# Four gate pieces behind the first values, rotation copies on two engines, urgent probability copies, and one store from another queue

## The chip, the cores and the metric

The kernel runs on one core of one Trainium2 chip. The time is device microseconds of one execution, the median of three runs: 883.94 us (883.38 to 884.23). The engines are TensorE (PE in the rows), VectorE (DVE), ScalarE (ACT), GpSimd (POOL) and SyncE (SP, which here only issues transfers). Each engine works through its own instructions in the order in which they stand; semaphores tie the engines together.

## The reference

Three layers over 256 tokens of width 1024, in float32:

```
# layer 1: retention
q, k, v, gate = split(x @ a_w_in); q, k = rope(q), rope(k) / 16
x = layer_norm(alpha * x + (norm(retention(q, k, v)) * silu(gate)) @ a_w_out)
# layer 2: latent attention, 16 heads
c = x @ kv_w_down; lat = rms_norm(c[:512]); k_rope = rope(c[512:])
k_nope, v = split(lat @ kv_w_up)
q_nope, q_rope = split(rms_norm(x @ b_w_in[:768]) @ b_w_uq); q_rope = rope(q_rope)
p = softmax(causal(q_nope @ k_nope + q_rope @ k_rope) * scale)
x = layer_norm(alpha * x + (p @ v * silu(x @ b_w_in[768:])) @ b_w_out)
# layer 3: recurrent branch and indexed sparse attention, gated, then a wide feed-forward
x = x + (gate0 * (y_rnn @ w_o_rnn) + gate1 * (y_attn @ w_o_attn)) @ w_out
x = x + square(relu(rms_norm(x) @ w_ff_in)) @ w_ff_out
```

`rope` turns pairs of columns: `x1 * cos - x2 * sin` and `x2 * cos + x1 * sin`.

## The kernel before, in words

All weights stream in as pieces of up to 128x1024 float32. A piece lands in a `raw` buffer (four of them; the small opening pieces land in `t` buffers). The helper `split` (L242) makes two halves of it in a `whl` buffer (eight of them): ScalarE casts it to the high half (L243), VectorE subtracts that from the piece for the low half (L244). Every product of matrices is then three matmuls, high by high, high by low and low by high (`mm3`, L297 to L299). Results gather in PSUM: four accumulators `acc`, two `tr` for transposes, two `att`. A new `acc` tile takes the buffer that falls free next in the program's order, and its first matmul waits until the last reader of that buffer is done.

The order of the instructions on each engine is set when the program is built, by a scheduler that follows the program's order and its own estimate of when things are ready; `urgent` (L208) lets a call go ahead of what is not urgent. Nothing is reordered while the program runs.

Four places matter here.

- **The opening** (`values_and_gates`, L509). Eight slices of the input each bring a piece of `x`, one of the first head's values (`av`) and one of its gates (`ag`). The values gather in two accumulators, the gates in two more, so all four are taken. The gate products of the last `CLOSE` slices are held back and run after the last value product. Then the values are copied out (`split`, named `t2r<-acc` in the rows), which frees an accumulator for the queries of head 0 (`ropeA("aq")`, matmuls `acc<-s,whl`).
- **The rotation in layer 2** (`ropeB`, L702). For the shared key once, and then for each of four groups of four heads. The accumulator `bqr` with the rotary queries is copied in four blocks of 32 partitions with neighbours exchanged (L708), multiplied by the cosines (L710) and sines (L713), and added (L714). L710 is the last reader of the accumulator. A group's `ropeB` stands among the last head's work of the group before.
- **The heads** (`head`, L731, and `mix`, L759). A head's probabilities are turned by three transposes into `tr` (L753), copied out as a high and a low part for the first 256 columns (`split`, L755, `t2r<-tr`) and as plain numbers for the last 128 (L756, `pair<-tr`); `mix` multiplies them with the values (`att<-t2r` and `att<-pair`, L764). Accumulators in a pair of heads are taken in the order `bqr` (first pair of a group only), `bqn`, `bkn`, `bv`, `bg`: the `bg` of a group's first pair takes the buffer that `bqr` had.
- **The end** (`ff_out`, L1255, and `store`, L1285). The last corner of the output is worked out in two halves of 256 columns in `tr` tiles. Each half is summed on VectorE (L1287) and stored (L1288); all five stores are issued from SP.

Of the kernel before, what the change touches and what calls it, by code (L numbers as in the profile page):

```python
# [31 lines left out]
WARM = 9  # L32
OPENING = tuple((k, 1) for k in range(8))
TABLES_AT = 3
CLOSE = 3
STEPS = ("w0 w1 b x0 G00 G01 x1 z0 g0 a x2 G02 z1 g1 a x3 G03 z2 g2 a x4 G04 z3 g3 a x5 G05 z4 g4 a x6 G06 z5 g5 "
         "a x7 G07 z6 g6 a G10 z7 g7 a G11 r G12 G13 a G14 G15 G16 G17 "
         "O00 O01 O02 O03 O04 O05 O06 O07 O10 O11 O12 O13 O14 O15 O16 O17").split()
# [110 lines left out]
def ff_group(g):  # L149
    return range(4) if g == 0 else range(2 * g + 2, 2 * g + 4)  # L150
# [21 lines left out]
def body(ctx, nc, tc, wpk, tabs, cols, rows, wab, xtok, out, start="A", stop="C"):  # L172
# [11 lines left out]
    dma = nc.sync.dma_start  # L184
    V = nc.vector
    A = nc.scalar
# [3 lines left out]
    def acc():  # L190
        return accp.tile([P, 512], F32, tag="acc", name="acc")

    def tr():
        return trp.tile([P, 512], F32, tag="tr", name="tr")

    def att():
        return attp.tile([P, 512], F32, tag="att", name="att")

    def t2():
        return t2p.tile([P, 512], F32, tag="t2", name="t2")  # L200

    def t2r():
        return t2p.tile([P, 512], F32R, tag="t2", name="t2r")

    def sm():
        return smp.tile([P, 16], F32, tag="sm", name="sm")

    def urgent(fn, *args):  # L208
        with tc.high_priority():
            fn(*args)  # L210
# [3 lines left out]
    def transpose(dst, src):  # L214
        flips.append(nc.tensor.transpose(dst, src, ident))  # L215
# [26 lines left out]
    def split(h, l, src):  # L242
        A.copy(h, src)  # L243
        V.tensor_sub(l, src, h.bitcast(F32))  # L244
# [39 lines left out]
    def take(name):  # L284
        for item in later:
            item[0] -= 1
        while later and later[0][0] <= 0:
            later.pop(0)[1]()
        while state["fetch"] < min(state["take"] + 1 + AHEAD, len(pieces)):
            fetch()  # L290
        state["take"] += 1
        got, pc = ready.pop(0)
        assert got == name, (got, name)
        return pc

    def mm3(ps, ah, al, bh, bl, st, sp):
        return [mm(ps, lhsT=ah, rhs=bh, start=st, stop=False),  # L297
                mm(ps, lhsT=ah, rhs=bl, start=False, stop=False),  # L298
                mm(ps, lhsT=al, rhs=bh, start=False, stop=sp)]  # L299
# [16 lines left out]
    def tgemm(name, npieces, act):  # L316

        ps = [None, None]
        k0 = 0
        for i in range(npieces):  # L320
            pc = take(name)
            for t in range(2):
                if i == 0:
                    ps[t] = acc()
                tpart(ps[t][:, :pc.n], pc, act, t, k0, i == 0, i == npieces - 1)
            k0 += pc.nk
        return ps
# [70 lines left out]
    def parts(st, j, i):  # L398

        n = st.shape[1] // 2  # L400
        return st[:, j * n + i * 128:j * n + i * 128 + 128]

    def half_product(ps, st, bh, bl, first=True):


        mm(ps, lhsT=st, rhs=bh, start=first, stop=False)  # L406
        mm(ps, lhsT=st, rhs=bl, start=False, stop=True)  # L407
# [13 lines left out]
    def row(name):  # L421

        i = [r[0] for r in ROWS].index(name)
        o = sum(r[1] for r in ROWS[:i])
        w = ROWS[i][1]
        got = []
        for c in range(0, w, 512):
            n = min(512, w - c)
            r = rowp.tile([P, 512], F32, tag="row", name="row")
            load(r[:, :n], rows[:, o + c:o + c + n])  # L430
            got.append(r[:, :n])
        return got
# [9 lines left out]
    def wide(ap, m):  # L442
        return ap.unsqueeze(1).to_broadcast([P, m, ap.shape[1]])
# [12 lines left out]
    if start == "A":  # L456
# [52 lines left out]
        def values_and_gates():  # L509
# [3 lines left out]
            for i, (k0, nk) in enumerate(OPENING):  # L513
                take("x")
                for nm in ("av", "ag"):
                    pc = take(nm)
                    if nm == "ag" and i >= len(OPENING) - CLOSE:
                        last.append((i, k0, pc))
# [77 lines left out]
    if start == "A":  # L596
        load(xs.rearrange("p t n -> p (t n)"), xtok.rearrange("p t n -> p (t n)"))
        g, b = row("lng0"), row("lnb0")
# [60 lines left out]
    if start in "AB":  # L659
# [37 lines left out]
        ps = tgemm("blat", 4, x1T)  # L697
# [4 lines left out]
        def ropeB(ps, m, dst):  # L702

            n = m * 256
            rot = t2()
            for i in range(4):
                a, b = 32 * i, 32 * (i ^ 1)
                A.copy(rot[a:a + 32, :n], ps[b:b + 32, :n])  # L708
            q = t2()
            V.tensor_mul(q[:, :n].rearrange("p (m n) -> p m n", m=m), ps[:, :n].rearrange("p (m n) -> p m n", m=m),  # L710
                         wide(cosB, m))
            r3 = rot[:, :n].rearrange("p (m n) -> p m n", m=m)
            V.tensor_mul(r3, r3, wide(sinB, m))  # L713
            V.tensor_add(dst, q[:, :n], rot[:, :n])  # L714
# [7 lines left out]
        ps = acc()  # L722
        ftile(ps[:, :256], take("bkr"), 0, x1T)
        ropeB(ps, 1, kr)
        A.copy(krh, kr)
        for j in range(2):
# [4 lines left out]
        def head(j, qn, qhl, qr, qs, pr, kn, khl, pl):  # L731
            c = slice(j * 128, j * 128 + 128)
            ck = slice(j * 256, j * 256 + 256)
            sc = att()
            mm(sc[:, 0:128], lhsT=qn[:, c], rhs=kn[:, c], start=True, stop=False)
            mm(sc[:, 0:128], lhsT=qr[:, pr * 256:pr * 256 + 128], rhs=krz[:, j], start=False, stop=True)
            mm3(sc[:, 128:384], qhl[:, 0, j], qhl[:, 1, j], khl[0][:, ck], khl[1][:, ck], True, False)
            half_product(sc[:, 128:384], parts(qs, j, pr), krh, krl[:, j], first=False)
            s = sm()
            pb = t2()  # L740
            for t, c in CT:
                V.tensor_tensor_reduce(out=pb[:, c], in0=sc[:, c], in1=maskB[:, c], scale=1.0,
                                       scalar=GONE, op0=ALU.add, op1=ALU.max, accum_out=s[:, t:t + 1])
            V.scalar_tensor_tensor(s[:, 2:4], s[:, 0:2], -1.0, sq, op0=ALU.mult, op1=ALU.mult)
            for t, c in CT:
                A.activation(out=pb[:, c], in_=pb[:, c], func=AF.Exp, scale=sq[:, t:t + 1],
                             bias=s[:, 2 + t:3 + t], accum_out=s[:, 4 + t:5 + t])
            V.reciprocal(s[:, 6:8], s[:, 4:6])
            for t, c in CT:
                V.tensor_scalar(pb[:, c], pb[:, c], s[:, 6 + t:7 + t], None, op0=ALU.mult)  # L750
            pp = tr()
            for i in range(3):
                transpose(pp[:, i * 128:i * 128 + 128], pb[:, i * 128:i * 128 + 128])  # L753
            pt = t2r()
            split(pt[:, 0:256], pt[:, 256:512], pp[:, 0:256])  # L755
            A.copy(pl, pp[:, 256:384])  # L756
            return pt, pl

        def mix(h, j, pt, vs, v, u):  # L759
# [9 lines left out]
        for g in range(4):  # L769
            if g == 1:  # L770
                softplus()
            ps = acc()
# [6 lines left out]
            for pr in range(2):  # L779
                ps = acc()  # L780
# [8 lines left out]
                ps = acc()  # L789
# [7 lines left out]
                ps = acc()  # L797
# [7 lines left out]
                ps = acc()  # L805
# [39 lines left out]
    if start in "AB":  # L845
        g, b = row("lng1"), row("lnb1")
# [129 lines left out]
    for g in range(4):  # L976
# [8 lines left out]
        for j in range(2):  # L985
            i = 2 * g + j
# [27 lines left out]
    for c in range(2):  # L1014
        ps = tgemm("cq", 4, hT)
# [239 lines left out]
    def ff_out(g):  # L1255
        hh = hid.pop(g)
        ms = range(len(ff_group(g)))
        pcs = [take("fo") for _ in ms]
        if g == NFG - 1:
            rest = t2()  # L1260
            V.scalar_tensor_tensor(rest, fps[1][1], r3[:, 1:2], xs[:, 1, 512:1024], op0=ALU.mult, op1=ALU.add)
        for t in range(2):
            tk = slice(t * 128, t * 128 + 128)
            for n in range(2):
                c = slice(n * 512, n * 512 + 512)
                corner = t == n == 1
                if corner and g == NFG - 1:
                    continue
                for m in ms:
                    mm3(fps[t][n], hh[:, 0, m, tk], hh[:, 1, m, tk], pcs[m].h[:, 0, c], pcs[m].l[:, 0, c],  # L1270
                        g == 0 and m == 0, g == NFG - 1 - corner and m == ms[-1])
                if g == NFG - 1:
                    store(t, c, fps[t][n], xs[:, t, c])
        if g < NFG - 1:
            return

        for i in range(2):
            c = slice(512 + i * 256, 768 + i * 256)
            ps = tr()[:, 0:256]
            for m in ms:  # L1280
                mm3(ps, hh[:, 0, m, tk], hh[:, 1, m, tk], pcs[m].h[:, 0, c], pcs[m].l[:, 0, c],
                    m == 0, m == ms[-1])
            store(1, c, ps, rest[:, i * 256:i * 256 + 256])

    def store(t, c, ps, x):  # L1285
        o = t2()[:, :c.stop - c.start]
        V.scalar_tensor_tensor(o, ps, r3[:, t:t + 1], x, op0=ALU.mult, op1=ALU.add)  # L1287
        dma(out[t * 128:t * 128 + 128, c], o)  # L1288
# [5 lines left out]
    for g in range(NFG):  # L1294
        if g + 1 < NFG:
            ff_in(g + 1)
        ff_out(g)
# [92 lines left out]
```

## Time and profile before

| what | value |
|---|---|
| median of three runs | 883.94 us |
| the profiled execution's own time | 884.91 us |
| its span, first to last instruction | 883.1 us |
| granted TensorE clock over the span | 0.999 |
| PE busy | 874.0 us (99%) |
| DVE busy | 621.1 us (70%) |
| ACT busy | 506.5 us (57%) |
| DMA, from HBM | 154.12 MB, 176 GB/s |

The page's span is shorter than the execution's own time by 1.8 us, which lie outside the first and the last instruction. In a timeline row the first number is the start in us from the beginning of the span, the second how long it took; `x3` means three instructions merged in one row; in brackets stands how long the engine had been idle before, and what ended that. `PE` rows are matmuls, which overlap: the distance between the starts of two of them is the time one takes from the engine.

### The profile page before, as it was taken

To read this page: it belongs to the slowest core of one execution; us is meant where nothing else is said; L and a number is where in the kernel's file an instruction comes from. 1 tells how busy PE (TensorE), PEld (TensorE's weight loads), DVE (VectorE), ACT (ScalarE), POOL (GpSimd) and SP (SyncE) were. 2 spreads that over 40 slices of the span, in tenths; PEclk is the share of its full clock that TensorE was granted. 3 is DMA by queue.
4 is the path that set the end of the run, shared out by engine and by line. 5 is a ranking of instruction groups with operands and counts; after the bars stand their busy time and mean duration, and the time that the engine had idled before them with its cause. 6 is when DMAs were issued, how large, how long until landed. Compare 5 with 4: busy or idle time off the path is not lost.

```text
span 883.1 us, 15178 instructions
## 1 busy us (share of the span) xinstructions
PE 874.0 (99%) x5845; PEld 801.1 (91%) x5845; DVE 621.1 (70%) x1175; ACT 506.5 (57%) x877; POOL 39.9 (5%) x45
## 2 busy tenths in 40 slices
PE   9999999999999999999999999999999999999998
PEld 6988898889999999999888899999999889999997
DVE  6886776757776777777588799777976756555552
ACT  6644445435756666576456678889643455444440
POOL 0000000100100000001311020000000000000000
PEclk9999999999999999999999999999999999999999
DMA  9855455734744444445555534333575556555531
GB/s 319 303 180 168 160 173 171 292 125 156 240 156 153 157 166 145 155 164 198 197 185 180 195 128 143 120 126 115 184 242 195 177 157 215 191 192 191 191 119 48
DMA packets 48313, 156.16 MB, mean 177 GB/s; under 512 B 5488, under 2 KB 7280, under 8 KB 48112
## 3 DMA queue, kind: packets, MB, share of 16 engines
q1 hardware_dynamic: 48240, 155.19, 51.9%
q8 instruction: 46, 0.75, 0.3%
q14 instruction: 27, 0.22, 0.1%
HBM read 154.12 MB, written 1.05 MB: 176 GB/s over the span
## 4 chain that ended last, share of the span: by engine, by line
PE 92%; DVE 5%; ACT 1%; issue 1%; DMA 1%; POOL 0%; SPq 0%; ACTq 0%; DVEq 0%
PE acc L297 24%; PE acc L299 24%; PE acc L298 24%; PE att L297 4%; PE att L298 4%; PE att L299 4%; PE tr L215 3%; DVE whl L244 1%; PE att L1071 1%; DVE s L998 1%; PE acc L1115 1%; DMA t<-wpk 1%; PE att L406 0%; PE att L407 0%; DVE sm L997 0%
## 5 line engine op out<-in xcount | busy, mean ns | idle before, releaser
L244 DVE TENSOR_TENSOR whl<-raw,whl 128x1024 fp32r<-128x1024 f32 (+1 forms) x278 | 327.0, 1187 | 137.0 <-ACT whl L243 135.5
L243 ACT CAST whl<-raw 128x1024 fp32r<-128x1024 f32 (+1 forms) x278 | 280.9, 1020 | 215.3 <-PE acc L299 100.9
L297 PE MATMUL acc<-s,whl 128*128 128x256 f32 x856 | 243.3, 284 | 0.7 <-DVE t2r L244 0.5
L299 PE MATMUL acc<-s,whl 128*128 128x256 f32 x856 | 241.5, 282 | 0.0
L298 PE MATMUL acc<-s,whl 128*128 128x256 f32 x856 | 241.4, 282 | 0.0
L298 PE MATMUL acc<-whl,s 128*128 128x512 f32 (+3 forms) x460 | 169.3, 369 | 0.0
L297 PE MATMUL acc<-whl,s 128*128 128x512 f32 (+3 forms) x460 | 168.5, 371 | 0.7 <-ACT s L243 0.5
L299 PE MATMUL acc<-whl,s 128*128 128x512 f32 (+3 forms) x460 | 169.1, 369 | 0.0
L297 PEld LDWEIGHTS acc<-s,whl 128*128 128x128 f32 x856 | 161.8, 189 | 2.3 <-DVE t2r L244 0.9
L298 PEld LDWEIGHTS acc<-s,whl 128*128 128x128 f32 x856 | 162.3, 190 | 0.5
L299 PEld LDWEIGHTS acc<-s,whl 128*128 128x128 f32 x856 | 161.6, 189 | 0.2
L297 PEld LDWEIGHTS acc<-whl,s 128*128 128x128 f32 x460 | 86.5, 188 | 15.3 <-ACT whl L243 1.8
L299 PEld LDWEIGHTS acc<-whl,s 128*128 128x128 f32 x460 | 86.6, 188 | 13.3
L298 PEld LDWEIGHTS acc<-whl,s 128*128 128x128 f32 x460 | 86.6, 188 | 12.6
L299 PE MATMUL att<-s,whl 128*128 128x256 f32 x224 | 62.9, 281 | 0.0
L297 PE MATMUL att<-s,whl 128*128 128x256 f32 x224 | 62.9, 281 | 0.0
L298 PE MATMUL att<-s,whl 128*128 128x256 f32 x224 | 62.9, 281 | 0.0
L297 PE MATMUL acc<-whl,hh 128*128 128x512 f32 x126 | 49.1, 390 | 0.0
L298 PE MATMUL acc<-whl,hh 128*128 128x512 f32 x126 | 49.0, 389 | 0.0
L299 PE MATMUL acc<-whl,hh 128*128 128x512 f32 x126 | 48.8, 390 | 0.0
L299 PEld LDWEIGHTS att<-s,whl 128*128 128x128 f32 x224 | 42.9, 191 | 0.1
L298 PEld LDWEIGHTS att<-s,whl 128*128 128x128 f32 x224 | 42.1, 188 | 0.5
(271 smaller groups left out, 1107.0 us busy)
## 6 DMA issues: line engine op xcount, KB each, us to landing
raw<-wpk SPq DMA_DIRECT2D x243, 512.0 KB, 4.1
raw<-wpk SPq DMA_DIRECT2D x32, 384.0 KB, 3.3
t<-wpk SPq DMA_DIRECT2D x16, 256.0 KB, 4.8
row<-rows SPq DMA_DIRECT2D x14, 256.0 KB, 6.0
raw<-wpk SPq DMA_DIRECT2D x4, 328.0 KB, 3.2
t<-wpk SPq DMA_DIRECT2D x8, 128.0 KB, 4.6
xs<-xtok SPq DMA_DIRECT2D x1, 1024.0 KB, 5.2
wb<-wab SPq DMA_DIRECT2D x4, 256.0 KB, 3.0
```

Of the source, the lines that this page charges most:

```text
L215: flips.append(nc.tensor.transpose(dst, src, ident))
L243: A.copy(h, src)
L244: V.tensor_sub(l, src, h.bitcast(F32))
L297: return [mm(ps, lhsT=ah, rhs=bh, start=st, stop=False), mm(ps, lhsT=ah, rhs=bl, start=False, stop=False), mm(ps, lhsT=al, rhs=bh, start=F ...
L298: mm(ps, lhsT=ah, rhs=bl, start=False, stop=False),
L299: mm(ps, lhsT=al, rhs=bh, start=False, stop=sp)]
L998: V.match_replace(out=score[:, c], in_to_replace=s[:, 0:8], in_values=score[:, c], imm_value=GONE)
L1071: mm(o[:, 0:256], lhsT=vC[:, 0, g, j], rhs=pts[j][:, 0:256], start=j == 0, stop=False)
L1115: mm(zz[:, i * 256:i * 256 + 256], lhsT=wb[(m % 4) // 2][:, o:o + 128], rhs=xc, start=True, stop=True)
```

## The change

The constant `CLOSE` goes from 3 to 4. In `ropeB` the first two of the four block copies stay on ScalarE, the other two go to VectorE. In `head` the copies of the turned probabilities are made urgent, and the plain copy now stands ahead of the split. The store of the second to last half of the corner is issued from ScalarE's queue.

```
-CLOSE = 3
+CLOSE = 4
...
                 a, b = 32 * i, 32 * (i ^ 1)
-                A.copy(rot[a:a + 32, :n], ps[b:b + 32, :n])
+                (A.copy if i < 2 else V.tensor_copy)(rot[a:a + 32, :n], ps[b:b + 32, :n])
...
             pt = t2r()
-            split(pt[:, 0:256], pt[:, 256:512], pp[:, 0:256])
-            A.copy(pl, pp[:, 256:384])
+            urgent(A.copy, pl, pp[:, 256:384])
+            urgent(split, pt[:, 0:256], pt[:, 256:512], pp[:, 0:256])
             return pt, pl
...
-            store(1, c, ps, rest[:, i * 256:i * 256 + 256])
-
-    def store(t, c, ps, x):
+            store(1, c, ps, rest[:, i * 256:i * 256 + 256], (nc.scalar.dma_start, dma)[i])
+
+    def store(t, c, ps, x, dma=dma):
```

The scheduler places much of layer 2 anew. Three places follow.

On ScalarE in the opening, the casts of weight pieces (`whl<-raw`) and the copies of the first values (`t2r<-acc`), before with a minus and now with a plus:

```order
-L243 CAST whl<-raw 128x1024 x4
-L243 CAST t2r<-acc 128x512 x2
-L243 CAST whl<-raw 128x1024
+L243 CAST whl<-t_263 128x512
+L243 CAST whl<-t_268 128x512
+L243 CAST whl<-raw 128x1024 x3
+L243 CAST t2r<-acc 128x512
+L243 CAST whl<-raw 128x1024
+L243 CAST t2r<-acc 128x512
```

The first values' copy stands behind three weight casts now, where it stood behind four.

On VectorE where group 3's `ropeB` begins (`acc_4010` is its `bqr`, `tr_3925` the turned probabilities of the last head of group 2), before:

```order
L244 TENSOR_TENSOR whl_4098<-raw_4096,whl_4098 128x1024 [waits DMAHW6_49,Activation_49]
L244 TENSOR_TENSOR t2r_3929<-tr_3925,t2r_3929 128x256 [waits Activation_49]
L766 SCALAR_TENSOR_TENSOR pair_3807<-att_3994,pair_3807 128x256 [waits PE_49]
L710 TENSOR_TENSOR t2_4063<-acc_4010,tab_1563 128x512 [waits Activation_49]
L713 TENSOR_TENSOR t2_4058<-t2_4058,tab_1563 128x512
```

and now:

```order
L244 TENSOR_TENSOR t2r_3929<-tr_3925,t2r_3929 128x256 [waits PE_49,Activation_49]
L708 COPY t2_4058<-acc_4010 32x512 [waits Activation_49]
L708 COPY t2_4058<-acc_4010 32x512
L710 TENSOR_TENSOR t2_4063<-acc_4010,tab_1563 128x512
L766 SCALAR_TENSOR_TENSOR pair_3807<-att_4002,pair_3807 128x256 [waits PE_49]
L713 TENSOR_TENSOR t2_4058<-t2_4058,tab_1563 128x512 [waits DVE_49]
```

Two copies have come in ahead of L710, and the first of them waits on a semaphore of ScalarE: the value it waits for is that of ScalarE's second L708 copy. (Between L766 and L713 one `whl<-raw` row is left out.)

On PE at the same place, from the last transposes of group 2 to the first `bg` matmul of group 3 (`acc_4245`, which takes the buffer of `acc_4010`), now:

```order
L215 MATMUL tr_3925<-ident_82,t2_3916 128x128 x2
L297 MATMUL acc_4159<-whl_3936,s5_1954 128x256
...
L299 MATMUL acc_4159<-whl_3936,s5_1954 128x256
L297 MATMUL att_4002<-t2r_3929,t2r_3877 128x256
L735 MATMUL att_4193<-pair_4119 128x128
L298 MATMUL att_4002<-t2r_3929,t2r_3877 128x256
L299 MATMUL att_4002<-t2r_3929,t2r_3877 128x256
L764 MATMUL att_4002<-pair_3807 128x128
L297 MATMUL acc_4245<-s0_1830,whl_3965 128x256
```

Between the last transpose and `acc_4245` stand 11 matmuls: 6 of `acc_4159` and the five `att` rows. Before there were 22. Where group 2 begins, the same count went from 46 to 23 (18 of them `acc`, and the same five `att` rows), where group 1 begins from 59 to 47, and where group 0 begins it is 95 both times. From a head's last transpose to the first matmul that reads its copied probabilities the count was 17 to 29 for the sixteen heads; now it is 18 to 30 for fourteen of them, 6 for the last head of group 2 and 3 for the fourteenth head, the second of group 3.

## Rows read from the trace of the kernel before

**Rows 1.** The page: its head and busy time by engine.

```profile
span 883.1 us, 15178 instructions
PE 874.0 (99%) x5845; PEld 801.1 (91%) x5845; DVE 621.1 (70%) x1175; ACT 506.5 (57%) x877; POOL 39.9 (5%) x45
```

**Rows 2.** What PE waited for: us in total, times, longest.

```profile
PE acc L297 <- DVE t2r L244: 0.5, 1, 0.5
PE att L764 <- ACT pair L756: 0.4, 1, 0.4
```

**Rows 3.** Timeline, opening, ACT.

```profile
25.44 1.05 ACT L243 CAST whl<-raw 128x1024 fp32r<-128x1024 f32 x1 [1.30 <-DVE whl L244]
26.40 1.07 ACT L243 CAST t2r<-acc 128x512 fp32r<-128x512 f32 x2
```

**Rows 4.** Timeline, opening, DVE.

```profile
26.52 1.23 DVE L244 TENSOR_TENSOR whl<-raw,whl 128x1024 fp32r<-128x1024 f32 x1 [1.12 <-ACT whl L243]
27.67 1.28 DVE L244 TENSOR_TENSOR t2r<-acc,t2r 128x512 fp32r<-128x512 f32 x2
```

**Rows 5.** Timeline, opening, PE.

```profile
27.51 0.39 PE L299 MATMUL acc<-whl,s 128*128 128x512 f32 x1
28.41 0.38 PE L297 MATMUL acc<-s,whl 128*128 128x256 f32 x1 [0.51 <-DVE t2r L244]
28.63 0.28 PE L298 MATMUL acc<-s,whl 128*128 128x256 f32 x1
```

**Rows 6.** Timeline, where group 3 begins, ACT.

```profile
376.69 0.37 ACT L243 CAST t2r<-tr 128x256 fp32r<-128x256 f32 x1 [0.64 <-PE tr L215]
377.08 2.35 ACT L708 COPY t<-acc 32x512 f32<-32x512 f32 x4
379.46 0.27 ACT L756 COPY pair<-tr 128x128 f32<-128x128 f32 x1
379.62 0.41 ACT L243 CAST s<-pair 128x256 fp32r<-128x256 f32 x1
```

**Rows 7.** The same place, DVE.

```profile
379.47 0.69 DVE L710 TENSOR_TENSOR t<-acc,tab 128x512 f32<-128x512 f32 x1 [1.62 <-ACT t L708]
380.07 0.68 DVE L713 TENSOR_TENSOR t<-t,tab 128x512 f32<-128x512 f32 x1
```

**Rows 8.** The same place, PE.

```profile
376.27 0.38 PE L215 MATMUL tr<-ident,t 128*128 128x128 f32 x2
...
378.62 0.28 PE L297 MATMUL att<-t2r 128*128 128x256 f32 x1
...
378.99 0.39 PE L735 MATMUL att<-pair 128*128 128x128 f32 x2
379.77 0.49 PE L764 MATMUL att<-pair 128*128 128x128 f32 x2 [0.40 <-ACT pair L756]
380.21 0.38 PE L297 MATMUL acc<-s,whl 128*128 128x256 f32 x1
380.44 0.28 PE L298 MATMUL acc<-s,whl 128*128 128x256 f32 x1
```

**Rows 9.** Timeline, where group 2 begins, ACT.

```profile
330.95 2.34 ACT L708 COPY t<-acc 32x512 f32<-32x512 f32 x4
```

**Rows 10.** The same place, DVE.

```profile
333.32 0.69 DVE L710 TENSOR_TENSOR t<-acc,tab 128x512 f32<-128x512 f32 x1 [1.30 <-ACT t L708]
```

**Rows 11.** The same place, PE: the transposes, and the first `bg` matmul.

```profile
330.13 0.38 PE L215 MATMUL tr<-ident,t 128*128 128x128 f32 x2
...
335.99 0.37 PE L297 MATMUL acc<-s,whl 128*128 128x256 f32 x1
```

**Rows 12.** Groups by form: a VectorE copy out of an accumulator.

```profile
L914 DVE COPY t<-acc 128x256 f32<-128x256 f32 x2 | 0.8, 414 | 0.0
```

**Rows 13.** The end: the last sum on DVE, the last store on SP, landing of stores.

```profile
879.86 0.48 DVE L1287 SCALAR_TENSOR_TENSOR t<-tr,tiny,t 128x256 f32<-128x256 f32 x1
880.38 0.37 SPq L1288 DMA_DIRECT2D out<-t  x1
DMA to landing us min/median/max: 1.9/2.0/2.1
```

## The prediction

> **What bounds the kernel now.** I read the page's busy times first: PE is busy for 874.0 us of 883.1, and no other engine passes 70% [rows 1]. So the time is PE's own work plus the few places where PE stands still, and an edit counts only if it removes or makes such a place. The list of what PE waited for shows which of them this change can touch: 0.5 us in the opening for the copied values, and 0.4 us in layer 2 for a probability copy [rows 2]. The timelines there give the true size, since a pause also counts the start-up of the first matmul after it.
>
> In the opening the last gate matmul starts at 27.51 and the first query matmul at 28.41 [rows 5]. The products before are 0.23 us apart (27.51 is one of a row of such starts), so the pause is 0.90 - 0.23 = 0.67 us; the next two starts are 0.22 apart where 0.12 is usual, another 0.10. Together 0.77 us. What it waits for is the first values' subtraction on VectorE, 27.67 to 28.36 [rows 4], which stands behind the weight piece at 26.52; and that waits for ScalarE's cast at 25.44, which had itself waited 1.30 us [rows 3].
>
> Where group 3 begins, the pause is longer than the list says. The three `att<-t2r` matmuls from 378.62 to 378.99 take 0.12 each, and a pair of small ones 0.22, so PE would have finished the L764 pair at 378.99 + 0.44 = 379.43; the first `bg` matmul starts at 380.21 [rows 8]. That is 0.78 us. Two waits end almost together: L764 waited for the plain copy at 379.46, which stood behind the four block copies on ScalarE [rows 6], and `bg` for L710, done at 379.47 + 0.69 = 380.16 [rows 7]. Taking the first away alone leaves the second where it is.
>
> Where group 2 begins there is no pause: L710 is done at 333.32 + 0.69 = 334.01 [rows 10], and `bg` starts at 335.99 [rows 11], 1.98 us later.
>
> **The change, part by part.** *CLOSE.* The value products end six matmuls earlier, 1.37 us at 0.23 each, and ScalarE's copy of the first values now stands ahead of the cast that waited until 25.44. Both it and its subtraction can then run behind the weight cast before that, so the accumulator is free by about 26, ahead of the 27.74 at which the held gates end. The six gate matmuls only move behind the values. The pause of 0.77 us goes. What is late next is the second values' copy, which still follows that cast; it frees the accumulator of the keys, and PE has two query pieces of 24 matmuls, 48 x 0.12 = 5.8 us, before it asks.
>
> *The chain through ropeB.* From the start of the last transposes to the `bg` matmul it took 380.21 - 376.27 = 3.94 us where group 3 begins [rows 8]. (Where group 2 begins, 330.13 to L710's end at 334.01 is 3.88; the same, without the 0.05 to PE [rows 10, 11].) The change does three things to this chain. It puts the plain copy ahead of the cast: +0.16, the distance of such a copy from the next instruction, 379.46 to 379.62 [rows 6]. It takes two block copies from ScalarE: 2 x 2.35 / 4 = -1.18 [rows 6, 9]. And it puts two copies on VectorE in front of L710. These wait for ScalarE's second copy, so they do not run beside it; the order shows that wait. The trace has no 32x512 copy on VectorE. A 128x256 copy out of an accumulator took 0.41 [rows 12]; a 128x512 operation from one took 0.69, and the next started 0.60 after it [rows 7]. Bounds for two: 0.60 (each at half the spacing, as if twice as fast) and 1.38 (no overlap). I take 1.20, the spacing, since the one VectorE copy that the trace has took what L710's row at double the columns lets expect. New chain: 3.94 + 0.16 - 1.18 + 1.20 = 4.12 us. It is not shorter; ScalarE is freed, the accumulator is not.
>
> *What PE has to do meanwhile.* This is what the scheduler moved, and it is the largest term. At group 3 the work between transposes and `bg` fell from 22 to 11 matmuls: 0.22 for the two transposes, 6 + 3 of 0.12, two pairs of 0.22, 1.74 us. The pause becomes 4.12 - 1.74 = 2.38, against 0.78 before: +1.60 us. At group 2 it fell from 46 to 23: 0.22 + (18 + 3) x 0.12 + 0.44 = 3.18 us, the pause 0.94, and before there was none; with 0.10 of slow start as in the opening, +1.04 us. At group 1, 47 matmuls are about 5.5 us and cover 4.12; at group 0, 95 do. The shared key's `ropeB` has blocks of 256 columns and no matmul takes its buffer so soon.
>
> *Urgent copies.* The wait for the plain copy at L764 goes, which is within the pause just counted. In exchange the cast comes 0.16 later for each head. The path from transposes to the first use is 376.69 - 376.27 = 0.42, + 0.16, + 0.37 for the cast [rows 6], + 0.05: 1.00 us. Heads with 18 or more matmuls between (2 us and up) hide it. The fourteenth has 3: 0.22 + 0.36 = 0.58, a new pause of 0.42, with the slow start +0.52 us. At the twelfth, with 6, the pause lies within group 3's.
>
> *The store.* The last store starts 0.04 after the last sum, 880.38 against 879.86 + 0.48 [rows 13], so the store before it doesn't hold it up on SP: there is nothing to gain. No store from ScalarE's queue is in the trace. If it lands like the others (1.9 to 2.1 us [rows 13]) it lands before the last; if it took 1 us longer, it would end the kernel some 0.7 us later. I take 0.
>
> Sum: -0.77 + 1.60 + 1.04 + 0.52 = **+2.4 us**. Against the profiled execution's own 884.91 that is 887.3; that execution lies 0.97 above the median of the runs shown, so for the median 883.94 + 2.4 = **886.3 us**. The rest of the order differs little, and PE's other pauses (the two layer norms, layer 3) stay.
>
> **Rivals.** (1) *The copies cost half.* If VectorE makes a block copy in 0.30, the chain is 3.52: the pauses become 1.78 and 0.34, the sum -0.77 + 1.00 + 0.44 + 0.52 = +1.2, 885.1 us. For it: ScalarE's 32-partition copies and VectorE's 128-partition ones say nothing direct on 32 partitions. Against it: on ScalarE 32 x 512 took 0.58, no less than what its columns ask.
>
> (2) *The two engines' copies run side by side.* Then L710 waits for 0.16 more, two copies of ScalarE and none of VectorE's: 3.94 + 0.16 - 1.18 = 2.92 us. Pauses 1.18 and none: -0.77 + 0.40 + 0.52 = +0.15, 884.1 us. Against it: the first VectorE copy waits for ScalarE in the order, and in the trace L710, which also only reads that accumulator, started 0.03 after ScalarE's last copy, though its engine had been idle 1.62 us [rows 6, 7]. [...]
>
> (3) *Not slower: both pauses go and nothing takes their place.* That asks that `bg` finds its accumulator free, so that PE has at least 4.12 us of work after the last transposes at both places. If the transposes of the twelfth head stood some 20 matmuls earlier for the chip than I count, -0.77 - 0.78 = -1.55, 882.4 us. For it: at group 3 both waits named in the profile are attacked. Against it: 11 matmuls stand there, and PE takes them in order.
>
> (4) *Worse.* The copies do not overlap (1.38, +0.18 at two places), the plain copy takes its whole 0.27 instead of 0.16 at three, and the store costs 0.5: +1.2 more, 887.5 us.
>
> **How the numbers follow.** Forecast 0.53, rival 1 0.2, rival 2 0.1, rival 3 0.1, rival 4 0.07. The bound for a difference is 0.2%, 1.8 us: faster means below 882.2, slower above 885.7. The forecast is 0.6 above that line and an error of that size is likely at times, so a fifth of it falls within; rivals 1 and 2 are within, rival 3 too but for a small part, rival 4 is slower. Slower 0.42 + 0.07 + a little of rival 1, together 0.55; faster 0.04; same 0.41. The range: rival 2 and what is slightly over it below, rival 4 above, 884.0 to 887.7 us; beyond it lie rival 3 and half of the extremes, two in ten.
>
> **What would show it.** Opening: the first query matmul 0.23 after the last gate matmul, some 0.8 us earlier than now. Groups 2 and 3: `bg`'s first matmul right behind L710's end, with PE idle about 0.9 and 2.4 us, and VectorE's two L708 rows behind ScalarE's two, 0.60 apart. The fourteenth head: its first `att` matmul 0.4 late behind the cast. End: the last store still 0.03 behind the last sum. The prediction is wrong if `bg` finds L710 long done, if VectorE's L708 starts with ScalarE's, or if the store from ScalarE lands after the last one.

## The result, and the profile after

The changed kernel takes **888.87 us** (median of 6 executions, 886.85 to 889.49) against 883.88 for the kernel before: ratio 1.0057, 95% interval 1.0048 to 1.0067. It is slower by 5.0 us (4.2 to 5.9); 2.4 had been forecast, with a range that ended at 887.7.

The page of the changed kernel, its head and the busy times [rows 1], from an execution of 888.92 us:

```profile
span 887.1 us, 15193 instructions
PE 875.4 (99%) x5845; PEld 803.0 (91%) x5845; DVE 628.4 (71%) x1185; ACT 501.0 (56%) x867; POOL 38.9 (4%) x45
```

PE does the same 5845 products. What it waited for in the changed kernel (us in total, times, longest), the rows that differ from [rows 2]:

```profile
PE acc L297 <- DVE t L710: 3.4, 2, 2.3
PE att L297 <- ACT t2r L243: 0.3, 1, 0.3
```

Both old waits of [rows 2] are gone, and two new ones are there. The opening first: the timeline of PE there, to be held against [rows 5].

```profile
27.78 0.39 PE L299 MATMUL acc<-whl,s 128*128 128x512 f32 x1
28.01 0.28 PE L297 MATMUL acc<-s,whl 128*128 128x256 f32 x1
28.13 0.28 PE L298 MATMUL acc<-s,whl 128*128 128x256 f32 x1
```

The first query product starts 0.23 behind the last gate product, the next 0.12 behind it: no pause and no slow start, as forecast.

Where group 2 begins, VectorE and PE [rows 10, 11]:

```profile
334.02 1.40 DVE L708 COPY t<-acc 32x512 f32<-32x512 f32 x2 [0.77 <-ACT t L708]
334.80 0.39 PE L764 MATMUL att<-pair 128*128 128x128 f32 x2
335.45 0.69 DVE L710 TENSOR_TENSOR t<-acc,tab 128x512 f32<-128x512 f32 x1
336.29 0.36 PE L297 MATMUL acc<-s,whl 128*128 128x256 f32 x1 [1.11 <-DVE t L710]
```

The L764 pair would be over at 334.80 + 0.22 = 335.02, so PE stands still for 1.27 us. VectorE's two copies wait for ScalarE's, take 1.40 together and hold L710 back. The same timeline where group 3 begins, all three engines [rows 6 to 8]:

```profile
377.95 0.38 PE L215 MATMUL tr<-ident,t 128*128 128x128 f32 x2
378.93 1.16 ACT L708 COPY t<-acc 32x512 f32<-32x512 f32 x2
379.76 0.38 PE L764 MATMUL att<-pair 128*128 128x128 f32 x2
380.13 1.40 DVE L708 COPY t<-acc 32x512 f32<-32x512 f32 x2 [0.76 <-ACT t L708]
381.56 0.69 DVE L710 TENSOR_TENSOR t<-acc,tab 128x512 f32<-128x512 f32 x1
382.40 0.55 PE L297 MATMUL acc<-s,whl 128*128 128x256 f32 x1 [2.26 <-DVE t L710]
382.75 0.41 PE L298 MATMUL acc<-s,whl 128*128 128x256 f32 x1
382.96 0.41 PE L299 MATMUL acc<-s,whl 128*128 128x256 f32 x1
...
385.73 0.28 PE L297 MATMUL acc<-s,whl 128*128 128x256 f32 x1
385.85 0.28 PE L298 MATMUL acc<-s,whl 128*128 128x256 f32 x1
```

The pause is 382.40 - (379.76 + 0.22) = 2.42 us. But look at the starts behind it: 382.75 and 382.96 are 0.21 apart, and only from 385.73 on is the distance 0.12 again. The table of windows says why. Behind a window stand its length, the busy us of PE, PEld (the loading of PE's weights), DVE, ACT and POOL, each with its number of instructions in brackets, then the granted clock, the DMA share and GB/s:

```profile
382.40:385.73 3.33, 3.33 (x15) 3.33 (x16) 2.85 (x5) 1.41 (x3) 0.00 (x0) 0.50 0.22 62
386.00:387.00 1.00, 1.00 (x11) 1.00 (x10) 1.00 (x1) 0.95 (x4) 0.00 (x0) 1.00 0.55 221
```

The granted clock is 0.50 for 3.33 us instead of 1.00, and in that time PE is busy throughout and gets through 15 products. At 0.12 each they are 1.74 us (15 x 0.116), so 1.59 us are lost **behind** the pause, where no list of waits shows them. (0.11 of that is a slow start that the old pause had too: 380.21 to 380.44 in [rows 8].)

The fourteenth head, PE:

```profile
408.18 0.28 PE L299 MATMUL acc<-s,whl 128*128 128x256 f32 x1
408.73 0.39 PE L297 MATMUL att<-t2r 128*128 128x256 f32 x1 [0.27 <-ACT t2r L243]
```

0.55 apart where 0.12 is usual: a pause of 0.43. And the end: the one store on ScalarE's queue, and the landing times of all of them [rows 13].

```profile
L1288 ACTq DMA_DIRECT2D out<-t x1: 374/374/374, 883.8 to 883.8; - x1
DMA to landing us min/median/max: 1.9/2.1/2.1
```

That store landed 2.1 us later, at 885.9, the last one, from SyncE, at 886.2.

### The profile page after: what moved, and what is told of

It reads as the page before. It is cut to its first block, busy times and chain, and to the rows that moved or that the text cites. A ratio compares the mean times of both kernels' runs of the same rounds, so it can differ in the third digit from the quotient of the medians.

```text
span 887.1 us, 15193 instructions
## 1 busy us (share of the span) xinstructions
PE 875.4 (99%) x5845; PEld 803.0 (91%) x5845; DVE 628.4 (71%) x1185; ACT 501.0 (56%) x867; POOL 38.9 (4%) x45
## 4 chain that ended last, share of the span: by engine, by line
PE 93%; DVE 5%; ACT 1%; issue 1%; POOL 0%; ACTq 0%; POOLq 0%
PE acc L297 25%; PE acc L299 25%; PE acc L298 25%; PE att L297 4%; PE att L298 4%; PE att L299 4%; PE tr L215 3%; DVE whl L244 1%; PE att L1071 1%; DVE s L998 1%; PE acc L1115 1%; PE att L406 0%; PE att L407 0%; DVE sm L997 0%; PE acc L453 0%
```

## The experiments

Theory A: the two copies on VectorE are the whole loss. They hold the accumulator longer, the scheduler reorders around that, PE stands still at groups 2 and 3, and the long pause costs the clock as well. The rivals are the urgent copies, VectorE as such, and a clock that falls for another reason. No run shows a clock in GHz: where an expectation gives one, it means what the traces show as a granted clock of 1.00 or 0.50.

**Four copies on ScalarE again** (the changed kernel, one part taken back):

```
-                (A.copy if i < 2 else V.tensor_copy)(rot[a:a + 32, :n], ps[b:b + 32, :n])
+                A.copy(rot[a:a + 32, :n], ps[b:b + 32, :n])
```

> The changed kernel with one part taken back: all four rotation copies are ScalarE's again; first values, urgent copies and store stay. Theory A, the copies on VectorE are the loss: with them back, 47 matmuls stand between the last transposes and the bg matmul at groups 2 and 3 (23 and 11 in the changed kernel) and 24 or more behind every head's transposes (3 at the fourteenth), so none of the three pauses of 1.3, 2.4 and 0.4 us appears, the old one of 0.8 goes too, and the clock stays at 2.4 GHz there. Before less 0.8 (opening) less 0.8: 882.3 us. Rival B, the urgent copies are the loss (each cast stands 0.16 later and its reader waits): pauses at the heads stay, 886 to 889 us. Rival C, each part carries some of it: 884 to 886 us.

Measured: 882.11 us against 883.80, ratio 0.9978 (0.9969 to 0.9987). Theory A gave 882.3. Its timeline where group 3 begins:

```profile
372.90 2.34 ACT L708 COPY t<-acc 32x512 f32<-32x512 f32 x4
375.27 0.69 DVE L710 TENSOR_TENSOR t<-acc,tab 128x512 f32<-128x512 f32 x1 [1.34 <-ACT t L708]
376.93 0.39 PE L764 MATMUL att<-pair 128*128 128x128 f32 x2
377.89 0.36 PE L297 MATMUL acc<-s,whl 128*128 128x256 f32 x1
```

L710 is over at 375.96, and bg comes 1.93 us later without a wait. The other three parts remain, and the kernel is faster than before: that puts the loss on the copies.

**The copies alone** (the kernel before with the opposite edit):

> The kernel before with only the third and fourth rotation copy moved to VectorE. Theory A: 22 matmuls stand before bg at group 2 and 5 at group 3, where the chain of 4.2 us then leaves pauses of 1.1 and some 3.4 us (0.8 before); with 0.1 of slow start that is +3.8, and with a clock at 1.2 GHz for a stretch behind the long one, which cost 1.5 us in the changed kernel, +5.3: 889.2 us. Without the clock's fall 887.7 us. Rival B, urgent copies are the loss: 884 us. VectorE's two copies stand 0.70 apart.

Measured: 890.38 against 883.80, ratio 1.0068 (1.0055 to 1.0081): the whole loss and more, since the two parts that gain are missing. Theory A's 889.2 lies within the interval (888.7 to 891.0). PE where group 3 begins, and the windows behind it:

```profile
379.16 0.49 PE L215 MATMUL tr<-ident,t 128*128 128x128 f32 x3
380.51 0.39 PE L297 MATMUL att<-t2r 128*128 128x256 f32 x1 [0.86 <-ACT t2r L243]
381.83 0.38 PE L298 MATMUL att<-t2r 128*128 128x256 f32 x1 [0.71 <-DVE t2r L244]
383.99 0.38 PE L297 MATMUL acc<-s,whl 128*128 128x256 f32 x1 [1.20 <-DVE t L710]
```

```profile
384.00:386.00 2.00, 2.00 (x11) 2.00 (x12) 2.00 (x5) 0.80 (x2) 0.00 (x0) 0.63 0.18 64
386.00:388.00 2.00, 2.00 (x12) 2.00 (x12) 1.42 (x3) 1.95 (x5) 0.00 (x0) 0.52 0.02 4
388.00:390.00 2.00, 2.00 (x20) 2.00 (x19) 1.94 (x5) 1.60 (x3) 0.00 (x0) 1.00 0.44 98
```

Here the standstill comes in three pieces with a few products between, and the clock falls all the same, a little later: 23 products in 4 us, and 20 in the 2 us after them.

**The urgent copies alone** (the two lines of the change in `head`):

> The kernel before with only the urgent probability copies. Theory A: 47 matmuls stand before bg at groups 2 and 3, all rotation copies are ScalarE's, the pause of 0.8 us at group 3 goes and no head has fewer than 24 matmuls to wait behind: 883.9 - 0.8 = 883.1 us. Rival B: casts that come 0.16 later cost at the heads, 885 us or more.

Measured: 882.36 against 883.80, ratio 0.9984 (0.9976 to 0.9993), 0.6 to 2.1 us faster. This part is a gain, and the wait of L764 [rows 2] is gone from PE's list; the 0.8 foretold lies within the interval.

**The first values alone** (`CLOSE = 4`):

> The kernel before with only the first values ending four pieces ahead. The pause of 0.77 us in the opening goes and nothing else moves: 883.1 us. The changed kernel was 1.1 to 1.2 us ahead by 50 us; if all of that belongs to this edit, 882.7 us; if the profile of before was slow there by chance, as its 884.9 against a median of 883.9 lets expect, 883.1 us or a little more.

Measured: 883.44 against 883.80, ratio 0.9991 (0.9982 to 0.9999): 0.1 to 1.6 us faster. The profile shows no pause in the opening; whether that is worth 0.4 or 0.8 the times do not tell.

**The store alone** (`(nc.scalar.dma_start, dma)[i]`):

> The kernel before with only the second to last store issued from ScalarE's queue. In the changed kernel that store landed 0.3 us before the last one, and the last was issued 0.03 behind its sum as before: 883.8 us, no change. If the second queue costs something at the end, 884.3 us or more; if the last store gains from it, 883.4 us.

Measured: 884.10 against 883.72, ratio 1.0003 (0.9994 to 1.0011). No change.

The profile of this run shows something about the opening, which this edit leaves as it was: `CLOSE` is 3, and ScalarE, VectorE and PE have the same order there as in the kernel before. The last cast ahead of the first values' copy, and PE [rows 3, 5]:

```profile
23.17 1.05 ACT L243 CAST whl<-raw 128x1024 fp32r<-128x1024 f32 x1 [0.22 <-DMA raw<-wpk]
27.07 0.39 PE L299 MATMUL acc<-whl,s 128*128 128x512 f32 x1
27.30 0.28 PE L297 MATMUL acc<-s,whl 128*128 128x256 f32 x1
```

The cast that started at 25.44 before starts at 23.17 here, and PE has no pause: 0.23 apart. Of the four profiles with `CLOSE = 3`, two have the pause (0.67 us in the kernel before, 0.78 with the urgent copies alone) and two have none (this one and the copies alone). The eight profiles with `CLOSE = 4` have none. So the pause comes in some executions only, and a gain below 0.77 from this part is what one should expect.

**The pause filled** (the changed kernel, in `mix`; `h == 11` is the twelfth head, the last of group 2):

```
             mm(o[:, 128:256], lhsT=v[:, c], rhs=pl, start=False, stop=True)
+            if h == 11:
+                for _ in range(16):
+                    mm(o[:, 256:512], lhsT=vs[:, c], rhs=pt[:, 0:256], start=True, stop=True)
```

> The changed kernel with 16 products more, whose result nobody reads, behind the eleventh head's last product: 16 x 0.115 = 1.8 us of work in the pause of 2.4 us where group 3 begins. Theory A, the clock fell because PE stood still so long: bg still starts 4.3 us after the last transposes, but its first products follow each other at 0.12 instead of 0.21 us, granted clock 2.4 GHz: 1.5 us less. The order behind the fourteenth head also changes (24 matmuls instead of 3 behind its transposes), so its pause of 0.44 goes: 888.9 - 1.5 - 0.4 = 887.0 us. Rival B, the clock falls there for another reason: the rows show 1.2 GHz again, 888.4 us. Rival C, the products delay VectorE's reader of that accumulator: 888.9 us or more.

Measured: 886.89 against 883.72, ratio 1.0039 (1.0027 to 1.0051); theory A gave 887.0. PE at the place, and the windows:

```profile
380.42 2.15 PE L767 MATMUL att<-t2r 128*128 128x256 f32 x16
382.92 0.36 PE L297 MATMUL acc<-s,whl 128*128 128x256 f32 x1 [0.35 <-DVE t L710]
383.11 0.28 PE L298 MATMUL acc<-s,whl 128*128 128x256 f32 x1
```

```profile
382.00:384.00 2.00, 1.65 (x14) 1.48 (x14) 1.97 (x4) 0.00 (x0) 0.00 (x0) 1.00 0.04 8
384.00:386.00 2.00, 2.00 (x20) 2.00 (x20) 1.86 (x5) 0.91 (x3) 0.00 (x0) 1.00 0.43 106
```

bg still waits for L710, but only 0.35 us; the clock stays at 1.00, and 20 products fit into 2 us. More work on PE made the kernel some 2 us faster (1.6 by the two ratios); some 0.4 of that is the fourteenth head's pause, which the moved order removed. All five executions had a mean granted clock of 0.999 or 1.000; the fall of 3.33 us to half would make it 0.998.

**A fifth copy on ScalarE, none on VectorE** (in the kernel with four on ScalarE):

```
-            for i in range(4):
+            for i in (0, 0, 1, 2, 3):
```

> No copy on VectorE: the kernel with four copies on ScalarE (882.1 us) and the first of them done twice, so five by ScalarE. Theory A, any longer hold of the accumulator makes the scheduler bring bg closer behind the transposes: 24 matmuls stand between them at group 2 and 12 at group 3, as with VectorE's copies, where there were 47 and 47. The chain is 4.1 + 0.58 = 4.7 us; pauses 4.7 - 3.3 = 1.4 and 4.7 - 1.9 = 2.8 us, 0.2 of slow starts, and the clock falls behind the long one as it did, 1.5: 882.1 + 5.9 = 888.0 us. Rival B, VectorE itself is the matter (its copies, its queue): a copy more on ScalarE costs 0 to 0.6 us, 882.1 to 882.7 us.

Measured: 888.83 against 883.72, ratio 1.0063 (1.0051 to 1.0075); theory A gave 888.0. Rival B, VectorE as the matter, is refuted: one ScalarE copy of 0.58 more costs 6.7 us against the kernel with four. The pauses are back; PE where group 3 begins:

```profile
379.38 0.38 PE L764 MATMUL att<-pair 128*128 128x128 f32 x2
380.28 0.49 PE L735 MATMUL att<-pair 128*128 128x128 f32 x2 [0.52 <-DVE pair L766]
383.10 0.38 PE L297 MATMUL acc<-s,whl 128*128 128x256 f32 x1 [2.33 <-DVE t L710]
383.31 0.29 PE L298 MATMUL acc<-s,whl 128*128 128x256 f32 x1
383.44 0.28 PE L299 MATMUL acc<-s,whl 128*128 128x256 f32 x1
```

What failed in theory A's expectation is the clock in this one execution: behind a longer standstill than the changed kernel's (0.68 and 2.49 us) the first two products are 0.21 apart, as after the old pauses (0.22 and 0.23 in [rows 5, 8]), and from the third on 0.12. This execution, at a mean granted clock of 1.000, took 887.46; the other four, at 0.996 to 0.998, took 888.76 to 890.37. So the length of the pause alone does not decide. By their mean clocks the other four had a fall, but they were not profiled, so its place in them is not shown.

**One copy on VectorE** (the changed kernel, `i < 3` for `i < 2`):

> The changed kernel with only the fourth rotation copy on VectorE. Theory A, pauses follow from the order: 47 matmuls at group 2 (no pause), 23 at group 3 (3.2 us of work against a chain of 4.3: pause 1.1, slow start 0.1), 3 behind the fourteenth head (0.5); the clock stays at 2.4 GHz, since the longest pause is 1.1: 882.1 + 1.7 = 883.8 us. Rival B, each copy on VectorE costs its share of the loss of 6.8 us against four on ScalarE: 885.5 us.

Measured: 884.37 against 883.72, ratio 1.0007 (0.9998 to 1.0015). Theory A gave 883.8; half the loss, 885.5, is above the interval (883.5 to 885.0). What PE waited for:

```profile
PE acc L297 <- DVE t L710: 1.0, 1, 1.0
PE att L297 <- ACT t2r L243: 0.3, 1, 0.3
```

One pause at group 3, none at group 2, and the fourteenth head's, as the order says. All its executions had a mean clock of 1.000.

**The changed kernel again**, to see how time goes with the clock:

> The changed kernel once more, to see how the time goes with the mean granted clock of each execution. Theory A (the fall of the clock behind the pause of 2.4 us costs 1.5 us and does not come in every execution): executions at 0.998 take 888.5 to 889.5 us, executions at 0.999 or 1.000 take 886.5 to 887.5, 1.5 to 2 us less; most are at 0.998. Rival B (the clock's fall is not what makes the difference): times at 0.998 and at 1.000 overlap, around 888.9 us.

Measured: 887.83 against 883.33, ratio 1.0054 (1.0040 to 1.0068). At a mean granted clock of 1.000: 887.07, 887.50 and 888.15 us; at 0.997 and 0.998: 887.27, 888.91 and 889.46. With the first six, the median is 887.3 for four executions at 1.000 and 888.9 for eight below: 1.6 us, as much as the rows of one profile gave. The two groups overlap: one execution at 0.997 took only 887.27. "Most at 0.998" held for eight of twelve. A mean does not say where the clock fell; the profile of this run, an execution of 888.91 at 0.998, shows it at the same place again:

```profile
382.40:386.50 4.10, 4.10 (x22) 4.10 (x23) 3.54 (x6) 2.15 (x4) 0.00 (x0) 0.58 0.39 117
```

**First values and urgent copies, no other part:**

> The kernel before with the first values four pieces ahead and the urgent copies, the store left on SyncE's queue. If the store is worth nothing, this is the kernel with four copies on ScalarE again: 882.1 us. If the store from ScalarE's queue gained or cost something there, 882.4 or 881.8 us.

Measured: 881.30 against 883.33, ratio 0.9980 (0.9972 to 0.9989). With the store it was 0.9978: no difference. This is the version to keep: it beats both kernels, and two of the change's four parts are all of its gain.

## Why the prediction was wrong, point by point

The direction and the mechanism of the pauses were right, the size was not: 2.4 forecast, 5.0 measured. By the steps of the sum:

- *What PE has to do meanwhile.* The step that failed. It priced a pause at its length and 0.10 of slow start, as the short pause of the opening had shown. Behind the pause of group 3, three times the longest that the trace of before has at these places, PE ran on at a granted clock of 0.50 and lost another 1.59 us (1.48 more than the slow start of before). No term, bound or rival held that, and so the range ended too low: without it the forecast stands 1 us below the executions in which the clock stayed (887.3), within the range. The filled pause shows that the fall hangs on the standstill: by the mean clock none in five executions, against eight in twelve without it. The repeated executions show that it does not come every time; what decides that stays open.
- *Group 3's pause.* Forecast 2.38, measured 2.42, though both of its parts were off: the chain took 382.40 - 377.95 = 4.45 instead of 4.12, and PE's work before it 2.03 instead of 1.74 because its `att` products came in pieces. That the two errors cancel is luck.
- *The chain through ropeB.* Mis-sized by 0.33, which group 2 shows by itself: pause 1.27 instead of 0.94. I took 1.20 for VectorE's two copies, from the distance of L710 and L713; they take 1.40, 0.69 each (median of the ten rows), the end of my bounds that rival 4 had: no overlap, and a copy costs no less than L710's operation on the same 512 columns, which took 0.69 as well. The rest is 0.03 around them and 0.10 from L710's end to PE. With 1.40 in the sum the pause of group 2 would have been forecast within 0.13.
- *Opening.* Mis-sized: the 0.77 was read from one profile and taken off the median of all executions, but two of the four profiles with `CLOSE = 3` have no such pause. The changed kernel has none, as forecast; the part's own run gave 0.1 to 1.6, 0.4 by the medians.
- *The fourteenth head.* Forecast a pause of 0.42, measured 0.43. *Store.* Forecast 0, measured 0.3 us (-0.5 to 1.0), no difference.
- *Rivals 1 and 2* fell with the row of the copies: they take full time and start 0.04 behind ScalarE's. Whether the two engines could read one accumulator side by side was not tried: the order has VectorE's first copy wait for ScalarE's second. *Rival 3*, that both pauses go, came true when VectorE's copies were left out.

By the rows: -0.77 + 1.64 + 1.37 + 0.53 + 1.48 = 4.3 us, at the lower end of the measured 4.2 to 5.9; with the opening at the 0.4 that its own run gave, 4.6. Without the clock's 1.48 that is 3.1, against 3.4 for the executions in which the clock stayed (887.3 against 883.9).

One thing the prediction left unexplained: why the work between transposes and bg shrank. The fifth copy answers it in part. It is no property of VectorE: one copy more on ScalarE, which holds the accumulator longer, takes the order from 47 and 47 matmuls to 24 and 12. Whether the scheduler answers to the hold or to the longer queue of an engine is not separated. A copy more of 0.58 us thus cost more than ten times its length.

## What to carry to other kernels

Where a scheduler sets the order, read the new order first and price each step that it lays bare: moving two copies to an idler engine did not shorten the chain, and the order that followed cost more than the chain. A pause of the engine that bounds the kernel is not priced by its length alone: look at the granted clock and the distance of the products behind it (here 0.50, and 0.21 us where 0.12 is usual), since that loss, here 1.59 us behind a pause of 2.42, appears in no list of waits. When several small edits come together, run each alone: here two gained, one did nothing, and one cost more than the others gave.

## What the runs showed of the hardware

One program gets different clocks in different executions: the changed kernel's means went from 0.997 to 1.000. Behind the pause of 2.4 us both of its profiles show the fall (a granted clock of 0.50 over 3.33 us in one, 0.58 over 4.10 us in the other); by the mean clock, eight of its twelve executions had a fall and four had none. Behind 3.2 us of standstill (0.68 and 2.49 with a pair of small products between) the profile of the fifth copy shows a granted clock of 1.00.

The pace of products differs at a granted clock of 1.00 too. The windows of the kernel with the first values alone, and of the kernel before, in a stretch that the edit does not touch:

```profile
640.00:660.00 20.00, 20.00 (x179) 20.00 (x178) 15.02 (x21) 8.76 (x10) 0.00 (x0) 1.00 0.70 236
```

```profile
640.00:660.00 20.00, 20.00 (x172) 20.00 (x171) 14.37 (x19) 8.73 (x9) 0.00 (x0) 1.00 0.74 250
```

PE is busy all the time at a granted clock of 1.00 in both, and gets through 179 products in one and 172 in the other: 0.8 us in a stretch of 20. Whether that goes with the execution or with the program the profiles do not tell, since both profiles of the changed kernel have 172. Single executions of the kernel with the first values alone took 881.14 to 884.54, a spread against which parts worth 0.4 to 0.8 us needed ten executions and more. What sets the pace stays open.
